# A list scheduler that hands out the lock between VectorE and GpSimd by turns

## The chip, the core and the metric

The kernel runs on one core of a Trainium2 chip. The core has five instruction queues: TensorE (PE), ScalarE (ACT), VectorE (DVE), GpSimd (POOL) and SyncE (SP); SP issues all DMA transfers here. Each queue is executed in the order in which it was written; between queues there are only semaphores. The time is the device time of one launch in microseconds. Each engine operates on tiles of 128 partitions; "128x512" is a tile of 512 float32 numbers in each partition.

## The reference

One encoder layer on a sequence of 2048 tokens with 1024 features, in float32. `mod` is six vectors from a conditioning vector c.

```python
mod = (silu(c) @ ada_w + ada_b)
sh1, sc1, g1, sh2, sc2, g2 = jnp.split(mod, 6, axis=-1)
h = rmsnorm(x, mix_norm_pre) * (1.0 + sc1) + sh1
y = windowed_gqa_sink(h, w_qkv, w_o, sink, rel_bias)     # 16 query heads, 4 key heads of 64
x = x + g1 * rmsnorm(y, mix_norm_post)
h = rmsnorm(x, ffn_norm_pre) * (1.0 + sc2) + sh2
a, b = jnp.split(h @ w_in, 2, axis=-1)                   # 2 x 2816
y = (silu(a) * b) @ w_out
x = x + g2 * rmsnorm(y, ffn_norm_post)
```

Attention works in blocks of 128 queries; each sees 384 keys (its own block and both neighbours), with a bias by relative position, and a learned extra logit in the softmax (the sink).

## The kernel before

**The work.** The sequence is cut into four chunks of 512 tokens (`NCH`), for the feed-forward part into two halves of 1024. Activations lie with features on partitions. A float32 matmul is made of three matmuls of the fp32r type: each operand is split into a high part (a cast by ACT, `hi`, or a cast of a weight, `w`) and a low part (the difference, mostly by DVE, `lo`), and high x high, high x low and low x high are added in one PSUM bank (`three`, `split`). So behind nearly each matmul of the kernel there are an ACT cast and a DVE subtraction of two inputs in SBUF.

The stages, in the order of time:

1. From 0 to about 170 us: the vectors of `mod` (40 loads `ada`, each reduced on DVE with `cb`, the broadcast conditioning vector), the norm of chunk 0, and the q, k, v projections of chunks 0 and 1. The normed input `x` becomes `hi` and `lo`; the weights are `wqkv` (raw) and `w`, or `wsr` and `ws` for the second part of the tiles.
2. To about 705 us: 64 attention units (score matmuls `bank<-k,q`, softmax on `pr` with running maximum `nm` and `rs`, value matmuls). Between them the scheduler places "fillers": the projections of chunks 2 and 3 (`fillers_qkv`), then the output projection (`fillers_o`, weights `wo`, activations `ol`) with residual and norm (`y`, `yacc`, `xacc`).
3. To about 800 us: the rest of the output projection. Results go to DRAM as `h2`; sums and differences of them (`hf`, written as `hd_d`) are operands of the next stage.
4. To about 1610 us: the hidden layer of the feed-forward part. Two by two blocks are multiplied in the manner of Strassen with seven products (`Block`, `Hidden`; `OPERANDS` names the blocks b11 to b22 and the sums t1 to t4 of the activations). Weights `wiri` are added up to `s_i` and split into `wa_i` and `ws_i`; results `p_i` and `u_i` are combined, partly on POOL.
5. To about 2050 us: the second matmul of the feed-forward part, again with seven products, in parts of 2 or 3 pairs of tiles (`PARTS`). Names end in `_o` here (`wiro`, `s_o`, `ws_o`, `wa_o`; `o1_0` is part 0 of half 1). The partial results are added up in the tiles `z`, partly by POOL. When the first half is complete, ACT squares its `z` (`zsq`), DVE adds the squares up (`zacc0` and `zacc1`, a chunk each), PE sums them over the partitions by a matmul with `ones` (`rstd_of`, named `nst`), and `zx` is written out.
6. The last chunks are normed and written (`finish`).

**The order.** The functions above don't issue instructions. Each call goes to a `Proxy`, and the `Recorder` (line 130) makes an `Op` of it, with its engine, the regions that it reads and writes, and its predecessors `pred`. `cost` (line 219) gives each `Op` a duration `occ` for its queue, a latency `lat` until its result may be used, and `port`, which says that it needs the lock which DVE and POOL share. `place` gives the tiles their addresses. `schedule` (line 537) then runs `ROUNDS` rounds. In each, `forward` (line 311) simulates the five queues with these durations: in a loop it takes the engine that can begin earliest, there the ready operation of the smallest `prio`, and adds it to the order; buffers of a tile go to the next that is to use them. An operation that needs the lock begins when the other engine's last locked operation has ended. From the second round on, an operation may be put back (up to four times, `o.put`) when a more urgent one, on its own engine or on the other side of the lock, will be ready before it would end. `backward` (line 477) takes the order of a round and works out the latest start of every operation, counted from the end; that is the `prio` of the next round. The round with the smallest simulated total is kept. `emit` (line 558) issues its order, inside `tc.manual_schedule()`, and the semaphores follow from the data alone. All instructions therefore have the line of `emit` in the profile, L594, and tiles tell them apart.

What `port` plans isn't enforced before: an order is fixed on each queue, but nothing says whether a DVE or a POOL operation goes first.

Of the kernel before, what the change touches and what calls it, by code (L numbers as in the profile page):

```python
# [19 lines left out]
P = 128  # L20
# [42 lines left out]

ROUNDS = 12

# [5 lines left out]

ENGINES = ("pe", "act", "dve", "pool", "sp")

class Op:
    __slots__ = ("i", "eng", "fn", "args", "kw", "reads", "writes", "occ", "lat", "port", "table", "tiles", "pred", "succ",
                 "start", "end", "put", "prio", "npred", "ready", "ins", "bytes")

# [52 lines left out]
class Recorder:  # L130
# [82 lines left out]
    def gap(self, q, op):  # L213

        if q.eng == op.eng == "pe":
            return 0
        return q.lat + (60 if q.eng != op.eng else 0)

    def cost(self, op, outs, ins):
# [6 lines left out]
        if eng == "sp":  # L226
            op.bytes = int(np.prod(outs[0].shape)) * 4
            op.occ, op.lat = 430, 0
        elif eng == "pe":
            if fn == "transpose":  # L230
                op.occ, op.lat = 108, 330
            elif outs[0].dtype == F32 and ins[0].dtype == F32:
                op.occ, op.lat = 860 * n // CH, 1060 * n // CH
            else:
                op.occ = n * 0.4167 + 13.5
                op.lat = op.occ + 200
        elif eng == "act":
            op.occ = n / 1.2 + (51 if psum else 93)
            op.lat = op.occ + 105
            if fn == "activation":  # L240
                if "accum_out" in op.kw:
                    op.occ, op.lat = op.occ + 93, op.lat + 93
                if isinstance(op.kw.get("scale"), bass.AP):
                    op.occ, op.lat = op.occ + 95, op.lat + 95
                f_ = op.args[2]
                op.table = {AF.Silu: "silu", AF.Ln: "log", AF.Exp: "log"}.get(f_)
        elif eng == "dve":
# [8 lines left out]
            if fn == "tensor_tensor_reduce":  # L256
                op.lat += 84
            op.port = n > P and (fast or len(sbuf) > 1)
        else:
            op.port = fn != "custom"  # L260
            if fn == "tensor_tensor":
                op.occ = n * 2.21 + 95
                op.lat = op.occ + 45
            elif fn == "custom":
                op.occ, op.lat = 1000, 1050
            else:
                op.occ = n * 1.05 + 153
                op.lat = op.occ + 35
# [42 lines left out]
    def forward(self, ahead):  # L311
# [8 lines left out]
        for o in ops:  # L320
            o.npred, o.ready, o.put = len(o.pred), 0.0, 0
# [3 lines left out]
        port = {"dve": 0.0, "pool": 0.0}  # L325
        lanes, dma, table = [0.0] * 8, 0.0, None
# [20 lines left out]
        def offer(o):  # L347
            ready = o.ready
            for b in o.tiles:
                if b.slot is None:  # L350
                    got = slot_of(b)
                    if got is None:
                        b.tag.parked.append(o)
                        return
                    ready = max(ready, got[1] + 60)
            heapq.heappush(soon[o.eng], (ready, o.prio, o.i, o))
# [18 lines left out]
        while n < len(ops):  # L375
            best = None
            for e in ENGINES:
# [18 lines left out]
            begin, e, o, src, item = best  # L396
            if e == "dve" and o.port and src is now[e] and begin > clock[e] + 150:
                other = [x for x in now[e] if not x[2].port]
                if other:
                    item = min(other)  # L400
                    o, begin = item[2], clock[e]
            if ahead and e in ("act", "dve", "pool") and o.put < 4:
                wait = 0.0
# [22 lines left out]
            for b in o.tiles:  # L426
                if b.slot is None:
                    got = slot_of(b)
                    if got is None:
                        again = True  # L430
                    elif got[1] + 60 > begin + 1e-6:
                        begin = got[1] + 60
# [18 lines left out]
            clock[e] = begin + o.occ  # L451
            o.start, o.end = begin, end
# [17 lines left out]
            for q in o.succ:  # L470
                q.npred -= 1
                q.ready = max(q.ready, begin if o.eng == q.eng == "pe" else end + (60 if o.eng != q.eng else 0))
                if not q.npred:
                    offer(q)
        return order, max(o.end for o in ops)

    def backward(self, order, total):


        after = {o: list(o.succ) for o in order}  # L480
        first = {}
        for o in order:
# [16 lines left out]
        late = {}  # L499
        lat = {o: o.lat if o.eng != "sp" else 2100 + o.bytes / 345.0 for o in order}  # L500
        for o in order:
# [3 lines left out]
        while left:  # L505
# [23 lines left out]
            for q in before[o]:  # L529
                g = 0 if q.eng == o.eng == "pe" else lat[q] + (60 if q.eng != o.eng else 0)  # L530
                limit[q] = min(limit[q], t - g + lat[q])
# [5 lines left out]
    def schedule(self, rounds):  # L537
# [6 lines left out]
        for i in range(rounds):  # L544
            order, total = self.forward(i > 0)
            if best is None or total < best[1]:
                best = order, total, {b: b.slot for b in self.bufs.values()}
# [5 lines left out]
        self.slots = best[2]  # L553
        return best[0]
# [3 lines left out]
    def emit(self, nc, tc, order, outside):  # L558
# [24 lines left out]
        banks = [nc.alloc_psum_tensor(f"bank{i}", [P, CH], F32).ap().tensor for i in range(BANKS)]  # L583
        table = None
        with tc.manual_schedule():
            for o in order:
# [6 lines left out]
                else:  # L593
                    getattr(engs[o.eng], o.fn)(*args, **kw)  # L594

# [1066 lines left out]
```

## Time and profile before

| | |
|---|---|
| median of three runs | 2072.3 us (2069.28 to 2074.15) |
| profiled execution | 2073.64 us, span 2071.9 us |
| mean granted clock of PE | 0.993 |
| busy PE, DVE, ACT, POOL | 2003.2, 1654.7, 1083.0, 744.2 us |
| instructions of PE, DVE, ACT, POOL in the profile | 9366, 2933, 2122, 687 |
| DMA | 396.35 MB, mean 191 GB/s |

An engine's busy time is the time in which it executes something. A row of a timeline gives the start, the length of a run of equal operations, what was done, and, in brackets, the idle time before it with the operation that ended the wait ("<-DVE ol" is the DVE operation that wrote `ol`). A DVE or POOL operation that waits for the lock appears in the trace as a longer operation and not as idle time. Tile names have their numbers left out.

### The profile page before, as it was taken

The page shows a single profiled execution, that of the slowest core. Times are in us where ns is not written, and L with a number is a line of the kernel's source. Part 1 is how long each engine was busy: PE and PEld are TensorE (multiplying, and loading weights), DVE is VectorE, ACT ScalarE, POOL GpSimd, SP SyncE. Part 2 cuts the span into 40 slices and gives each one's busy share as a digit, 9 for nine tenths or more (in the row PEclk, how much of TensorE's full clock was granted, in tenths as well). Part 3 has the DMA queues.
Part 4 walks back from the last instruction along what each step waited for, and adds up shares of the span by engine and source line. Part 5 has one row for each costly group of instructions (what it writes and reads, how often), then busy time and mean ns, then how long its engine had stood idle before and what let it go on. Part 6 is the DMA issues. An engine that isn't in the chain of part 4 may idle for free.

```text
span 2071.9 us, 29065 instructions
## 1 busy us (share of the span) xinstructions
PE 2003.2 (97%) x9366; PEld 1661.6 (80%) x9366; DVE 1654.7 (80%) x2933; ACT 1083.0 (52%) x2122; POOL 744.2 (36%) x687
## 2 busy tenths in 40 slices
PE   6999999999999999999999999999999999999997
PEld 4787888888778778788888888888888788877786
DVE  6666877765668889897988999776666789999998
ACT  5546776677778864343443533333334744465432
POOL 2403544466989723433445322222221000240031
PEclk9999999999999999999999999999999999999999
DMA  8896865676777794444456744423323544437443
GB/s 279 277 319 205 253 215 179 196 250 240 241 264 240 238 363 166 164 154 160 163 172 223 275 143 164 142 95 107 112 99 120 173 162 144 138 112 276 171 153 107
DMA packets 200516, 396.35 MB, mean 191 GB/s; under 512 B 20091, under 2 KB 62124, under 8 KB 195244
## 3 DMA queue, kind: packets, MB, share of 16 engines
q1 hardware_dynamic: 199788, 393.97, 56.6%
q8 instruction: 74, 1.21, 0.2%
q14 instruction: 78, 0.64, 0.1%
q10 hardware_dynamic: 576, 0.52, 0.1%
HBM read 270.65 MB, written 123.76 MB: 190 GB/s over the span
## 4 chain that ended last, share of the span: by engine, by line
PE 74%; DVE 12%; DMA 5%; ACT 3%; POOL 3%; issue 2%; SPq 1%; DVEq 0%; ACTq 0%; POOLq 0%
PE bank L594 74%; DVE z L594 3%; DMA ada<-ada_w 1%; SPq L594 1%; DVE ws_o L594 1%; POOL pr L594 1%; POOL y L594 1%; POOL z L594 1%; DMA zx<-x_d 1%; DVE ada L594 1%; DMA k_d<-e 1%; DVE wa_o L594 1%; DMA ol<-o_d 1%; DVE s_o L594 1%; DVE zacc L594 1%
## 5 line engine op out<-in xcount | busy, mean ns | idle before, releaser
L594 PE MATMUL bank<-ht,ws_i 128*128 128x512 f32 x1584 | 373.8, 389 | 0.0
L594 PEld LDWEIGHTS bank<-ht,ws_i 128*128 128x128 f32 x1584 | 297.3, 188 | 61.7
L594 PE MATMUL bank<-hb,wa_i 128*128 128x512 f32 x1056 | 254.2, 389 | 0.0
L594 PEld LDWEIGHTS bank<-hb,wa_i 128*128 128x128 f32 x1056 | 198.2, 188 | 41.4 <-ACT hb L594 0.2
L594 PE MATMUL bank<-ol,wo 128*128 128x512 f32 x768 | 206.6, 398 | 3.3 <-DVE ol L594 2.2
L594 POOL TENSOR_SCALAR pr<-pr,rs 128x384 f32<-128x384 f32 (+1 forms) x256 | 150.8, 607 | 126.2 <-DVE rs L594 122.2
L594 ACT ACTIVATE pr<-pr,nm 128x385 f32<-128x385 f32 (+1 forms) x256 | 155.0, 606 | 71.5 <-DVE nm L594 66.5
L594 ACT CAST ws_i<-s_i 128x512 fp32r<-128x512 f32 x132 | 82.0, 621 | 206.8 <-PE bank L594 129.7
L594 POOL TENSOR_TENSOR z<-z,z 128x512 f32<-128x512 f32 x32 | 63.3, 1999 | 349.6 <-issue 159.0
L594 DVE CUSTOM_DVE_ANT_0 pr<-bank,bias,nsink 128x384 f32<-128x384 f32 (+1 forms) x256 | 148.6, 596 | 44.4 <-PE bank L594 41.2
L594 POOL TENSOR_TENSOR p_i<-p_i,u_i 128x512 f32<-128x512 f32 x44 | 71.8, 1634 | 290.2 <-ACT wa_i L594 132.6
L594 DVE TENSOR_TENSOR u_i<-bank,u_i 128x512 f32<-128x512 f32 x176 | 120.6, 686 | 66.5 <-PE bank L594 65.9
L594 PEld LDWEIGHTS bank<-ol,wo 128*128 128x128 f32 x768 | 143.2, 189 | 30.7 <-DVE ol L594 2.6
L594 DVE TENSOR_TENSOR plo<-bank,phi 128x512 fp32r<-128x512 f32 x184 | 120.0, 685 | 37.4 <-ACT phi L594 35.3
L594 PE MATMUL bank<-k,q 128*128 128x384 f32 (+1 forms) x512 | 132.1, 345 | 5.3 <-DVE nm L594 5.2
L594 PE MATMUL bank<-hi,ws 128*128 128x512 f32 x384 | 137.1, 404 | 0.0
L594 ACT CAST wa_i<-wiri 128x512 fp32r<-128x512 f32 x132 | 81.4, 620 | 102.5 <-PE bank L594 102.2
L594 PE MATMUL bank<-hb,ws_i 128*128 128x512 f32 x528 | 128.7, 393 | 3.2 <-ACT p_i L594 3.2
L594 DVE TENSOR_TENSOR wa_i<-wiri,wa_i 128x512 fp32r<-128x512 f32 x132 | 113.8, 862 | 21.6 <-ACT wa_i L594 21.6
L594 PE MATMUL bank<-ht,wa_i 128*128 128x512 f32 x528 | 126.8, 389 | 0.0
L594 PEld LDWEIGHTS bank<-hb,ws_i 128*128 128x128 f32 x528 | 100.1, 190 | 25.0 <-ACT p_i L594 4.0
L594 PEld LDWEIGHTS bank<-ht,wa_i 128*128 128x128 f32 x528 | 99.1, 188 | 20.6
(245 smaller groups left out, 4511.8 us busy)
## 6 DMA issues: line engine op xcount, KB each, us to landing
wiri<-w_in SPq DMA_DIRECT2D x88, 512.0 KB, 4.7
ada<-ada_w SPq DMA_DIRECT2D x40, 512.0 KB, 5.5
wiro<-w_out SPq DMA_DIRECT2D x48, 384.0 KB, 3.7
q_d<-e SPq DMA_DIRECT2D x64, 256.0 KB, 3.8
q<-q_d SPq DMA_DIRECT2D x16, 1024.0 KB, 5.6
wo<-wo_d SPq DMA_DIRECT2D x16, 1024.0 KB, 6.2
g_d_b<-p_i SPq DMA_DIRECT2D x44, 256.0 KB, 4.7
g_d_t<-p_i SPq DMA_DIRECT2D x40, 256.0 KB, 2.0
```

The lines of the kernel that those rows point to most:

```text
L594: getattr(engs[o.eng], o.fn)(*args, **kw)
```

## The change

1. The lock in `forward`. Before, the engine that can begin first takes it. Now `ask` holds the time at which an operation would begin without the lock; among operations with the same `begin` the one that asked first is taken, so the two engines alternate when both wait. An operation may begin 60 ns ahead of the end of the other's.
2. Real dependences. An operation that is put back because of one on the other side of the lock remembers it (`o.wait = y`). If `y` has by then been scheduled and the operation would otherwise start no later than 20 ns after it, `o.extra = [y]`: its simulated start is after the end of `y`, and `emit` adds a dependence with `tc.add_manual_dep`, so that it waits for `y` by a semaphore. `backward` counts these edges too. In the built kernel there are 43 of them: in 31 a POOL operation waits for a DVE one, in 12 a DVE operation for a POOL one.
3. Durations and delays of the model. In place of 60 ns from one engine to another stand 55, 50, 35, 105 and 30 (`HOP`, by the waiting engine), and 30 within an engine. The latency of a matmul falls by 38; activations with a bias per partition get 95 more, POOL's additions 30 more, DVE's additions on 64 partitions 97 more. DMAs get a time on the wire by their bytes at 408 or 330 instead of 345 bytes per ns, issue times of 385 to 650 instead of 430, and a completion of 450 or 750 instead of 900; all clocks start at 700.
4. 18 rounds in place of 12. A method `replay` is added, which nothing calls.

The recorded operations and their counts on each engine are the same before and after (9352 on PE, 2935 on DVE, 1872 on ACT, 692 on POOL, 1228 on SP), and so is the arithmetic of each. The order differs: on DVE 1910 operations stand at another place in the queue (by 3.3 places in the mean, 65 at most), on PE 2064 (1.4, 156 at most), on ACT 942, on POOL 226 (11 at most) and on SP 660 (2.2, 32 at most).

```diff
-ROUNDS = 12
+ROUNDS = 18
+HOP = {"pe": 55, "act": 50, "dve": 35, "pool": 105, "sp": 30}
@@ gap
-        return q.lat + (60 if q.eng != op.eng else 0)
+        return q.lat + HOP[op.eng] if q.eng != op.eng else q.lat + 30
@@ cost
-            op.occ, op.lat = 430, 0
+            parts, run = outs[0].ap[0][1], min(self.run(x) for x in outs + ins)
+            op.wire = op.bytes / (0.408 if run >= 2048 and parts == P else 0.33) / 1e3
+            op.occ, op.lat = 650 if parts == DH or run * 2 * P == op.bytes else 385 if run >= 2048 else 450, 0
-                op.lat = op.occ + 200
+                op.lat = op.occ + 162
...
+            if outs[0].ap[0][1] == DH and fn == "tensor_tensor":
+                op.occ, op.lat = op.occ + 97, op.lat + 10
...
-                op.occ = n * 2.21 + 95
+                op.occ = n * 2.21 + 125
@@ forward
-        clock = dict.fromkeys(ENGINES, 0.0)
+        clock = dict.fromkeys(ENGINES, 700.0)
...
+                ask = begin
                 if o.port:
-                    begin = max(begin, port["pool" if e == "dve" else "dve"])
-                if best is None or begin < best[0]:
-                    best = begin, e, o, src, item
+                    begin = max(begin, port["pool" if e == "dve" else "dve"] - 60)
+                if best is None or (begin, ask) < best[:2]:
+                    best = begin, ask, e, o, src, item
...
-                            wait = max(wait, r + (y.occ if g != e else 1.0))
+                            w = r + (y.lat + HOP[e] if g != e else 1.0)
+                            if w > wait:
+                                wait, by = w, y if g != e else None
                 if wait:
                     drop(src, o)
                     o.put += 1
+                    if by is not None:
+                        o.wait = by
...
+            y = o.wait
+            if y is not None and y.npred < 0 and max(clock[e], o.ready) <= y.start + 20:
+                o.extra = [y]
+                begin = max(begin, y.end + HOP[e])
...
             if e == "sp":
                 lanes.sort()
                 begin = max(begin, lanes[0])
+                late = 150 * (lanes[3] > begin)
                 first = max(begin + 1200, dma)
-                dma = first + max(o.bytes / 345.0, 100.0)
-                end = dma + 900
+                dma = first + max(o.wire, 80.0) + {2: 500, 3: 1600}.get(moved, 0)
+                moved += 1
+                end = dma + (450 if o.out else 750)
...
@@ backward
+        for o in order:
+            for q in o.extra:
+                after[q].append(o)
@@ emit
+        sync = mybir.DependencyInfo(mybir.DependencyClass.Sync, mybir.DependencyReason.DATA)
...
+                for q in self.extra.get(o, ()):
+                    tc.add_manual_dep(o.ins.ins, q.ins.ins.name, sync, reason="turn")
```

More of the change, by code (lines that the diff above doesn't have):

```diff
@@ L450, in forward @@
                     port[e] = begin + o.occ
-            clock[e] = begin + o.occ
+            o.npred = -1
+            clock[e] = begin + o.occ + (late if e == "sp" else 0)
             o.start, o.end = begin, end
@@ L475, in forward, with replay @@
         return order, max(o.end for o in ops)
+    def replay(self, order):
+        queues = {e: [o for o in order if o.eng == e] for e in ENGINES}
+        at = dict.fromkeys(ENGINES, 0)
+        clock = dict.fromkeys(ENGINES, 700.0)
+        port, moved = {"dve": 0.0, "pool": 0.0}, 0
+        lanes, dma, table = [0.0] * 8, 0.0, None
+        after, seen = {}, set()
+        need = {}
+        for o in order:
+            o.npred, o.ready = len(o.pred), 0.0
+            edges = list(o.extra)
+            for b in o.tiles:
+                if b not in seen:
+                    seen.add(b)
+                    edges += [q for x in b.before for q in x.ops if q is not o]
+            o.npred += len(edges)
+            for q in edges:
+                after.setdefault(q, []).append(o)
+        n = 0
+        while n < len(order):
+            best = None
+            for e in ENGINES:
+                if at[e] == len(queues[e]):
+                    continue
+                o = queues[e][at[e]]
+                if o.npred:
+                    continue
+                begin = max(clock[e], o.ready, lanes[0] if e == "sp" else 0.0)
+                ask = begin
+                if o.port:
+                    begin = max(begin, port["pool" if e == "dve" else "dve"] - 60)
+                if best is None or (begin, ask) < best[:2]:
+                    best = begin, ask, e, o
+            begin, ask, e, o = best
+            at[e] += 1
+            if e == "act" and o.table and o.table != table:
+                table = o.table
+                begin += 1283
+            if e == "sp":
+                late = 150 * (lanes[3] > begin)
+                first = max(begin + 1200, dma)
+                dma = first + max(o.wire, 80.0) + {2: 500, 3: 1600}.get(moved, 0)
+                moved += 1
+                end = dma + (450 if o.out else 750)
+                lanes[0] = end
+                lanes.sort()
+            else:
+                end = begin + o.lat
+                if o.port:
+                    port[e] = begin + o.occ
+            clock[e] = begin + o.occ + (late if e == "sp" else 0)
+            o.start, o.end = begin, end
+            n += 1
+            for q in o.succ + after.get(o, []):
+                q.npred -= 1
+                q.ready = max(q.ready, begin if q.eng == e == "pe" else end + (HOP[q.eng] if q.eng != e else 30))
+        return max(o.end for o in order)
@@ L499, in backward @@
         late = {}
-        lat = {o: o.lat if o.eng != "sp" else 2100 + o.bytes / 345.0 for o in order}
+        lat = {o: o.lat if o.eng != "sp" else 1950 + o.wire for o in order}
         for o in order:
```

46 lines of the change are left out of this document (29 added, 17 removed).

## The prediction, made before the changed kernel was run

> **What bounds the kernel now.** I read the page's head first, then the chain that ended last, then the windows by stage, and last the timeline of TensorE (PE), because PE decides nearly everything here.
>
> ```profile
> span 2071.9 us, 29065 instructions
> PE 2003.2 (97%) x9366; PEld 1661.6 (80%) x9366; DVE 1654.7 (80%) x2933; ACT 1083.0 (52%) x2122; POOL 744.2 (36%) x687
> PE 74%; DVE 12%; DMA 5%; ACT 3%; POOL 3%; issue 2%; SPq 1%; DVEq 0%; ACTq 0%; POOLq 0%
> ```
>
> PE is busy 2003.2 of 2071.9 us, so all its idle time is 68.7 us. The change keeps every matmul; it can only shrink or enlarge that idle time and the stretches of lower clock that follow it. The windows show where it lies (columns: window, length, busy us and count of PE, PE weight loads, VectorE (DVE), ScalarE (ACT), GpSimd (POOL); granted clock; DMA share; GB/s):
>
> ```profile
> 0.00:50.00 50.00, 29.33 (x97) 19.77 (x98) 35.34 (x54) 25.52 (x34) 12.48 (x11) 1.00 0.80 278
> 150.00:200.00 50.00, 47.06 (x212) 38.84 (x211) 33.36 (x69) 34.09 (x69) 14.65 (x18) 0.93 0.70 223
> 550.00:600.00 50.00, 44.72 (x218) 35.83 (x218) 31.31 (x76) 37.54 (x82) 46.87 (x51) 0.97 0.71 236
> 700.00:750.00 50.00, 46.71 (x207) 37.53 (x206) 39.81 (x42) 31.74 (x48) 23.53 (x15) 1.00 0.97 347
> 800.00:850.00 50.00, 47.84 (x204) 39.09 (x203) 44.78 (x54) 18.17 (x32) 24.71 (x16) 0.97 0.46 163
> 1800.00:1850.00 50.00, 49.85 (x220) 40.97 (x219) 47.73 (x87) 30.20 (x61) 19.66 (x5) 1.00 0.48 159
> 1850.00:1900.00 50.00, 41.88 (x168) 31.75 (x168) 45.99 (x74) 34.04 (x64) 4.80 (x4) 0.97 0.74 256
> 1900.00:1950.00 50.00, 47.62 (x210) 39.11 (x210) 47.96 (x89) 22.92 (x46) 0.00 (x0) 1.00 0.55 191
> ```
>
> The startup loses 20.67 us of PE time. After it, five stages lose something: 150 to 200 (2.94), 550 to 600 (5.28), 700 to 750 (3.29), 800 to 850 (2.16) and 1850 to 1950 (8.12 + 2.38). From 1800 on DVE is busy 46 to 48 of 50 us, so there it stands next to PE as a bound. The waits themselves, in the timeline of PE (start, us, work; in brackets the idle time before it and who ended it):
>
> ```profile
> 24.28 2.08 PE L594 MATMUL bank<-hi,w 128*128 128x512 f32 x4 [9.26 <-ACT hi L594]
> 175.86 0.80 PE L594 MATMUL bank<-k,q 128*128 128x256 f32 x2 [2.70 <-DVE nm L594]
> 573.32 0.62 PE L594 MATMUL bank<-k,q 128*128 128x384 f32 x2 [2.27 <-DVE nm L594]
> 728.94 1.40 PE L594 MATMUL bank<-ol,wo 128*128 128x512 f32 x5 [2.25 <-DVE ol L594]
> 840.18 4.61 PE L594 MATMUL bank<-hb,ws_i 128*128 128x512 f32 x12 [2.15 <-ACT p_i L594]
> 862.15 3.04 PE L594 MATMUL bank<-hb,ws_i 128*128 128x512 f32 x12 [1.00 <-ACT p_i L594]
> 1858.01 2.07 PE L594 MATMUL bank<-zacc,ones 128*128 128x512 f32 x2 [3.27 <-DVE zacc L594]
> 1893.06 2.11 PE L594 MATMUL bank<-ht2o,ws_o 128*128 128x512 f32 x8 [1.82 <-ACT z L594]
> 1924.35 0.73 PE L594 MATMUL bank<-hb11o,wa_o 128*128 128x512 f32 x2 [2.38 <-ACT wa_o L594]
> ```
>
> The same twelve matmuls take 4.61 us after the wait at 840 and 3.04 us after the one at 862: some waits are followed by a slow stretch, worth 1.6 us there. The windows' clock agrees: (1 - 0.97) x 50 = 1.5 us in three of them, (1 - 0.93) x 50 = 3.5 us in 150 to 200.
>
> **The change, part by part.** It removes and adds no instruction. Every engine issues the same operations in another order, and 43 dependences are new: 31 times a POOL operation waits for a DVE one, 12 times the reverse. The order of the built kernels gives the moves used below. The other edits (18 rounds, new delays and durations in the planner's model, the unused `replay`) have no cost on the chip beyond the order that they lead to. So I go stage by stage, with each price bounded by idle plus slow clock from the rows above.
>
> *Startup.* These rows are of ACT and PE:
>
> ```profile
> 22.76 0.81 ACT L594 ACTIVATE x<-x,mod,coef 128x512 f32<-128x512 f32 x1 [4.87 <-DVE coef L594]
> 23.61 0.62 ACT L594 CAST hi<-x 128x512 fp32r<-128x512 f32 x1
> 27.42 0.94 ACT L594 CAST w<-wqkv 128x896 fp32r<-128x896 f32 x1 [0.37 <-DMA wqkv<-w_qkv]
> 34.28 1.89 PE L594 MATMUL bank<-lo,w 128*128 128x512 f32 x7 [1.42 <-DVE lo L594]
> 49.42 1.20 PE L594 MATMUL bank<-lo,w 128*128 128x512 f32 x4 [1.17 <-DVE lo L594]
> 55.96 1.20 PE L594 MATMUL bank<-lo,w 128*128 128x512 f32 x4 [1.49 <-DVE lo L594]
> 61.58 1.20 PE L594 MATMUL bank<-lo,w 128*128 128x512 f32 x4 [0.54 <-DVE lo L594]
> ```
>
> The new ACT order has the casts of weights w0_1 and w0_2 ahead of the first scaled activation x0_0 and its cast to `hi`. The cast at 27.42 is w0_2; it waited for its DMA. If that weight lands when it does now, `hi` ends at 27.42 + 0.94 + 0.81 + 0.62 = 29.8 instead of 23.61 + 0.62 = 24.2: PE starts 5.6 later. The head of the queue thus blocks x0_0, hi0_0 and the first matmul behind it. But four later waits, 1.42 + 1.17 + 1.49 + 0.54 = 4.6 us, are for data that arrive at their own pace, and they shrink by as much: net +1.0. On DVE three operations of the modulation (`ada`) move ahead of the norm, which frees their buffers and lets SP issue the next loads earlier. If the weights then land before ACT wants them, PE starts as now and the four waits go: -4.6. If nothing is absorbed, it is +5.6. I take +1.0, since weight and waits are both measured.
>
> *173 us.* ACT stands on one cast:
>
> ```profile
> 172.65 1.05 ACT L594 CAST ws<-wsr 128x1024 fp32r<-128x1024 f32 x1 [5.00 <-DMA wsr<-w_qkv]
> 175.06 0.50 ACT L594 ACTIVATE pr<-pr,nm 128x257 f32<-128x257 f32 x1
> ```
>
> For 5.00 us this cast of ws8 waited for its DMA, with two softmax activations queued behind it, and PE's scores behind these. The new order puts both activations and one `e` ahead of it. The wait of 2.70 should go but for one softmax activation of 0.50: -2.2. I keep the slow clock, as nothing shows it gone. Ends: 0 (the DMA is as late and something else stands behind it) and -(2.70 + 3.5) = -6.2.
>
> *566 to 616 us.* One row of DVE, for the price of an operation without contention:
>
> ```profile
> 832.55 0.68 DVE L594 TENSOR_TENSOR s_i<-wiri 128x512 f32<-128x512 f32 x1
> ```
>
> POOL is busy 46.87 of 50 us, with the same operations afterwards. A better order cannot lift that; four of the new edges (y, yacc) make POOL wait for a DVE operation here. Four times 0.68 would be +2.7; the other end is all idle and slow clock, -(5.28 + 1.5) = -6.8. I take -1.0, near zero, because the bound stays.
>
> *711 to 732 us.* PE waits for `ol`, whose load was issued late:
>
> ```profile
> 719.42 0.89 SPq L594 DMA_DIRECT2D ol<-o_d  x1
> 717.25 1.78 DVE L594 TENSOR_TENSOR hf<-y,hf 128x512 f32<-128x512 f32 x1
> 724.57 1.05 ACT L594 CAST ol<-ol 128x1024 fp32r<-128x1024 f32 x1 [1.63 <-DMA ol<-o_d]
> ```
>
> SP issues in order, and the load of ol3_3 stood behind writes of `h2` and `hd_d_t`, whose sources come from DVE operations stretched to 1.78 us. In the new SP order it stands seven places earlier, ahead of these writes; DVE's own part stands eight places earlier. Eight operations of 0.68 are 5.4 us, more than the 2.25 that PE waits, so the wait goes; the writes are then late, and no one on PE reads them soon. -2.3; ends 0 and -3.3 (all idle of the window).
>
> *825 to 862 us.* Here DVE and POOL take turns already:
>
> ```profile
> 829.14 1.78 DVE L594 TENSOR_TENSOR wiri<-wiri 128x512 f32<-128x512 f32 x1
> 830.33 1.75 POOL L594 TENSOR_TENSOR ly<-ly,lr 128x512 f32<-128x512 f32 x1
> ```
>
> This row of DVE is the last of three alike from 825.75 on: 1.78 instead of 0.68 made DVE 3.3 late, and through weights and casts `p_i` was late at 840 and 862. The planner now foresees this and two of the new edges (ly2_2, wa12_i0_5 after POOL operations) lie here. Ends: -(2.15 + 1.00 + 1.5) = -4.7, and two more such turns, 2 x 1.1 = +2.2. I take -2.0, a little nearer to the gain, the weight splits having been moved for it.
>
> *1835 to 1925 us.* This is the largest pool after the startup:
>
> ```profile
> 1835.42 14.71 POOL L594 TENSOR_TENSOR z<-z,z 128x512 f32<-128x512 f32 x2 [10.47 <-DVE z L594]
> 1847.18 0.55 DVE L594 TENSOR_TENSOR wiro<-wiro 128x384 f32<-128x384 f32 x1
> 1848.91 1.15 ACT L594 ACTIVATE zsq<-z 128x512 f32<-128x512 f32 x2 [2.63 <-POOL z L594]
> 1924.92 1.09 PE L594 MATMUL bank<-ht2o,ws_o 128*128 128x512 f32 x4
> 1925.85 0.39 PE L594 MATMUL bank<-hb11o,wa_o 128*128 128x512 f32 x1
> ```
>
> POOL's first `z` was ready at 1835.42, and the two took 14.71 us where one takes 1.75 above: DVE ran weight splits without a pause until 1847.7 and only then did POOL end. From there the way is POOL z, ACT zsq, DVE zacc, then PE's norm matmul with 3.27 idle. In the new order the two sums zacc end 25 and 31 places earlier on DVE, with the splits of o1_0_2 and o1_0_3 behind them, and the norm matmul stands 64 matmuls earlier on PE (the last two rows put four matmuls at 0.93 us, 0.23 each, and 64 at 14.7). Ends: -(8.12 + 2.38 + 1.5) = -12.0 when the chain flows, and 14.7 less the 1.82 at 1893 that it would absorb = +12.9 when `z` comes as late as now and PE stands at the earlier place. I take -3.0: the wait of 3.27 goes, and those up to 1925 stay, since DVE is as full as before.
>
> The sum is 1.0 - 2.2 - 1.0 - 2.3 - 2.0 - 3.0 = -9.5. The profiled execution took 2073.64 us, 1.3 above the median of the three runs (2072.3); 2073.64 - 9.5 = 2064.1, and against the median 2062.8.
>
> [...]
>
> **The rivals.**
>
> *First, slower: the norm chain is starved at its new place.* POOL's `z` must win the lock between DVE operations that stand back to back; at 1835 it lost for over 12 us. DVE now has zacc between splits and, standing in order, would itself stop until `z` is through, at 47.73 of 50 us busy. PE's norm matmul is fixed 14.7 us earlier. It decides when `z` is over 5 us late there. Price +12.9 in place of -3.0: 2062.8 + 15.9 = 2078.7. For it speaks the row at 1835; against it that the new edges give POOL's z0_1_5 and z0_3_4 a fixed place behind a DVE operation, and that DVE leaves the lock free while it waits for zsq.
>
> *Second: the startup's delay isn't absorbed.* Then +5.6 in place of +1.0: 2067.4. For it speaks that the ACT queue is in order; against it the four waits of 4.6.
>
> *Third: the new waits take back what the moves give.* 43 edges at 0.68 are 29 us, at 1.78 they are 77. DVE and POOL carry 12 + 3 = 15% of the chain that ended last, so some 4.4 to 11.5 us lie on the path: 2067.2 to 2074.3, in the middle 2071, no change that can be measured. For it speaks that a wait between full engines is seldom free; against it that POOL is 36% busy overall and most of its edges are in the hidden stage, where PE loses little.
>
> **How the numbers follow.** A measurement of this kernel tells about 0.2% (4.1 us) from no change, so "same" is 2068.2 to 2076.4. Forecast (2056 to 2068): 0.38. First rival (2076 to 2084): 0.22. Second (2065 to 2071): 0.12, of which 0.05 faster and 0.07 same. Third (2067 to 2079): 0.28, of which 0.03 faster, 0.12 same and 0.13 slower. Faster 0.46, same 0.19, slower 0.35. The range 2053 to 2082 leaves some 0.08 at each side; the forecast's own is 2056 to 2068.
>
> **What would show it.** Right: the first matmul near 29 us and shorter waits for `lo` until 62; no 5 us wait of ACT for wsr near 173; no `ol` wait at 729; POOL's `z` of 1.3 to 1.8 us each near 1835 and the norm matmul without idle time. Wrong: PE's idle time above 68.7 us, a `z` of POOL over 5 us with PE waiting behind zacc, or POOL waits in 550 to 620 longer than now.

## The result, and the profile after

The changed kernel takes 2088.3 us (median; 2085.7 to 2089.1), the kernel before 2073.2 us (2069.3 to 2075.7): a ratio of 1.0071, with a 95% interval of 1.0058 to 1.0084. It is slower by 15 us (0.7%), where 10 us faster had been forecast. The profiled execution took 2085.66 us, 12.0 more than the one of before (2073.64); its span is 11.6 longer.

The head of the page after, and the shares of its chain:

```profile
span 2083.5 us, 29084 instructions
PE 2003.7 (96%) x9366; PEld 1664.8 (80%) x9366; DVE 1639.4 (79%) x2933; ACT 1082.6 (52%) x2122; POOL 726.0 (35%) x687
PE 71%; DVE 10%; DMA 10%; issue 3%; ACT 2%; POOL 2%; SPq 1%; DVEq 0%; ACTq 0%; POOLq 0%
```

PE does the same work, so its idle time grew from 68.7 to 79.8 us. DVE and POOL are busy for 15.3 and 18.2 us less, 33.5 us together, with the same operations. A wait for the lock counts as busy time: before, 128x512 operations of DVE from 825.75 to 829.14 us, beside POOL's, took 1.76 to 1.78 us, and 0.68 at 832.55, with POOL idle; the ends of the two engines' operations alternate there (DVE 827.51, POOL 828.67, DVE 829.21, POOL 830.37). By these sums the engines wait less for each other: the change does on them what it says. But the share of DMA in the chain that ended last has doubled, from 5% to 10%. The windows of after (columns as in the prediction):

```profile
150.00:200.00 50.00, 41.99 (x183) 34.34 (x182) 32.94 (x64) 32.83 (x63) 13.81 (x15) 0.93 0.81 255
550.00:600.00 50.00, 44.80 (x212) 35.66 (x211) 29.47 (x73) 34.71 (x75) 45.84 (x50) 0.90 0.65 225
700.00:750.00 50.00, 46.59 (x215) 37.68 (x214) 38.62 (x51) 37.57 (x65) 25.72 (x22) 0.97 0.81 287
850.00:900.00 50.00, 47.04 (x200) 38.00 (x199) 39.16 (x54) 17.94 (x30) 22.52 (x16) 0.97 0.44 149
1850.00:1900.00 50.00, 39.92 (x161) 31.22 (x161) 43.40 (x76) 29.70 (x57) 3.33 (x2) 0.93 0.66 219
1900.00:1950.00 50.00, 50.00 (x223) 41.39 (x222) 49.80 (x92) 25.64 (x54) 0.00 (x0) 1.00 0.56 202
```

The window from 150 to 200 lost 5 us more of PE time than before (41.99 busy against 47.06). The one from 550 to 600 is as idle as before, but at a clock of 0.90 instead of 0.97. From 1850 to 1900 more is lost and from 1900 to 1950 all is regained. The timeline of PE, with the waits that matter:

```profile
28.14 0.79 PE L688 MATMUL bank<-hi,w 128*128 128x512 f32 x1 [14.06 <-ACT hi L688]
88.60 0.47 PE L688 MATMUL bank<-nhia,ones 128*128 128x512 f32 x1 [2.75 <-DVE nhia L688]
169.39 0.39 PE L688 MATMUL bank<-k,q 128*128 128x256 f32 x1 [2.43 <-DVE e L688]
176.63 0.58 PE L688 MATMUL bank<-k,q 128*128 128x256 f32 x1 [5.58 <-DVE nm L688]
583.28 1.01 PE L688 MATMUL bank<-k,q 128*128 128x384 f32 x2 [2.27 <-DVE nm L688]
723.63 1.64 PE L688 MATMUL bank<-ol,wo 128*128 128x512 f32 x6 [3.26 <-DMA wo<-wo_d]
798.53 0.50 PE L688 MATMUL bank<-nhilo,ones 128*128 128x512 f32 x1 [1.73 <-DVE nhilo L688]
895.37 0.49 PE L688 MATMUL bank<-nhil,ones 128*128 128x512 f32 x1 [2.10 <-DVE nhil L688]
1856.09 0.70 PE L688 MATMUL bank<-zacc,ones 128*128 128x512 f32 x1 [2.25 <-DVE zacc L688]
1878.02 1.22 PE L688 MATMUL bank<-hb11o,wa_o 128*128 128x512 f32 x2 [7.41 <-ACT wa_o L688]
```

Both kernels issue the same number of matmuls, so the start of the n-th one can be compared in the two traces (the first has number 0). That places the loss without asking which wait is whose:

| n-th matmul | before, us | after, us | later by |
|---|---|---|---|
| 300 | 94.19 | 95.51 | 1.3 |
| 600 | 152.66 | 154.11 | 1.4 |
| 900 | 219.94 | 226.58 | 6.6 |
| 2550 | 530.31 | 538.35 | 8.0 |
| 3000 | 625.93 | 636.59 | 10.7 |
| 3600 | 748.11 | 759.15 | 11.0 |
| 4200 | 889.50 | 902.90 | 13.4 |
| 7500 | 1639.70 | 1651.66 | 12.0 |
| 8700 | 1926.98 | 1939.75 | 12.8 |
| 9364 (last but one) | 2058.80 | 2070.35 | 11.6 |

The largest step, 5.2 us, is the start of the attention between 150 and 220 us, where a wait was expected to vanish. These rows of ACT, POOL and DVE of after lead to PE's wait of 5.58:

```profile
156.35 0.58 ACT L688 CAST e<-bank 128x512 fp32r<-128x512 f32 x1 [3.65 <-DMA q_d<-e]
172.27 1.33 ACT L688 ACTIVATE nsq<-x 128x512 f32<-128x512 f32 x2 [1.37 <-DMA x<-xT]
172.97 1.26 POOL L688 TENSOR_TENSOR nacc<-nacc,nsq 128x512 f32<-128x512 f32 x1 [3.11 <-ACT nsq L688]
174.27 0.69 DVE L688 TENSOR_TENSOR nacc<-nacc,nsq 128x512 f32<-128x512 f32 x1 [2.56 <-POOL nacc L688]
176.09 0.48 DVE L688 CUSTOM_DVE_ANT_0 pr<-bank,bias,nsink 128x256 f32<-128x256 f32 x1
```

At 156 ACT stands for 3.65 us, because the buffer `e` (there are two) is still being written out to `q_d`. The operations on the second half of chunk 2 stand behind it and release the buffers for the loads of chunk 3 later. At 172 ACT waits for the last of these loads; its square goes to POOL's sum and then to DVE's, and only behind that sum in DVE's queue stands `pr`, the softmax step which also gives the maximum `nm` that PE's next score matmul waits for. The cast of `ws8` that held ACT before isn't in this chain any more.

The same chain stood in the kernel before, 5 to 6.5 us earlier; ACT waited there for `q_d` too, for longer, but at 140 us:

```profile
140.33 0.60 ACT L594 ACTIVATE e<-bank 128x512 fp32r<-128x512 f32 x1 [4.47 <-DMA q_d<-e]
167.03 0.63 ACT L594 ACTIVATE nsq<-x 128x512 f32<-128x512 f32 x1 [0.93 <-DMA x<-xT]
167.76 0.69 DVE L594 TENSOR_TENSOR nacc<-nacc,nsq 128x512 f32<-128x512 f32 x1 [1.67 <-ACT nsq L594]
```

So what changed first is when the transfers come, and not how long they take in a crowd. The view of DMA (issues, KB each, median us from issue to landing) shows it: its stretch from 144 to 157 us of after, from 134 to 146 us of before, and from 130 to 145 us of e10, the fastest kernel of those below.

```profile
DMA packets 3248, 4.92 MB, mean 378 GB/s; under 512 B 181, under 2 KB 2460, under 8 KB 3247
bias<-tab_d SPq DMA_DIRECT2D x3, 768.0 KB, 9.0
k_d<-e SPq DMA_DIRECT2D x4, 256.0 KB, 7.7
q_d<-e SPq DMA_DIRECT2D x2, 256.0 KB, 8.9
```

```profile
bias<-tab_d SPq DMA_DIRECT2D x4, 768.0 KB, 8.1
q_d<-e SPq DMA_DIRECT2D x5, 256.0 KB, 7.6
```

```profile
bias<-tab_d SPq DMA_DIRECT2D x4, 768.0 KB, 7.5
q_d<-e SPq DMA_DIRECT2D x2, 256.0 KB, 10.0
```

The bias loads, 768 KB each, were issued from 134.6 us on before, from 142.7 us on after, and from 129.7 us on in e10. The writes around and behind them are slow in all three (`q_d` 7.6, 8.9 and 10.0 us, against 3.7 in the median of the whole kernel of after). Before, this crowd was ending when the loads of chunk 3 and the writes of k came, from 148.5 us on; these then took 4.1 and 4.4 us:

```profile
k_d<-e SPq DMA_DIRECT2D x7, 256.0 KB, 4.4
x<-xT SPq DMA_DIRECT2D x6, 256.0 KB, 4.1
```

After, the writes of k fall into it, and the last load of chunk 3 is issued at 168.76 us instead of 163.24.

Over the whole kernel, by the last part of the page of after, the medians are

```profile
wiri<-w_in SPq DMA_DIRECT2D x88, 512.0 KB, 4.7
q_d<-e SPq DMA_DIRECT2D x64, 256.0 KB, 3.7
wo<-wo_d SPq DMA_DIRECT2D x16, 1024.0 KB, 5.9
g_d_t<-p_i SPq DMA_DIRECT2D x40, 256.0 KB, 2.0
```

Worked out from the code for a transfer with nothing ahead of it, the figures that the planner holds against the first three are:

| | 256 KB write | 512 KB load | 1024 KB load |
|---|---|---|---|
| before (345 bytes per ns, 900 ns) | 2.9 | 3.6 | 5.1 |
| changed (408 or 330, 450 or 750 ns) | 2.4 | 3.2 | 4.5 |
| median in the trace of after | 3.7 | 4.7 | 5.9 |
| tried below (300, 1500 ns) | 3.6 | 4.4 | 6.2 |

Against these three medians both models are too short, and the change makes the DMA part worse. But what a transfer takes depends on its place here (writes of 256 KB landed in 8.9 us in the stretch of `q_d` above, in 3.7 in the median of all `q_d`, and those of `g_d_t` in 2.0, in both kernels), and the planner also puts one transfer behind another (`first = max(begin + 1200, dma)`), so this is no direct comparison. The fairer test is the whole plan. Its own total, which the planner's code gives when it is run, is 2033.1 us for the changed kernel and 2025.4 for the one before: the traces' spans are 50 and 46 us longer. In e10 (300 bytes per ns and 1500 ns) it is 2053.9, and the span 7 us longer. The changed kernel's plan has the four bias loads land 6.4 to 9.8 us after their issue, as in the trace (6.5 to 9.8). What it has wrong there is the time: the first is issued at 126.1 us in the plan and at 142.7 in the trace (before 124.0 and 134.6, in e10 130.8 and 129.7).

### The profile page after: what moved, and what is told of

Its sections match the earlier page's. It is cut to its first block, busy times and chain, and to the rows that moved or that the text cites. A ratio compares the mean times of both kernels' runs of the same rounds, so it can differ in the third digit from the quotient of the medians.

```text
span 2083.5 us, 29084 instructions
## 1 busy us (share of the span) xinstructions
PE 2003.7 (96%) x9366; PEld 1664.8 (80%) x9366; DVE 1639.4 (79%) x2933; ACT 1082.6 (52%) x2122; POOL 726.0 (35%) x687
## 4 chain that ended last, share of the span: by engine, by line
PE 71%; DVE 10%; DMA 10%; issue 3%; ACT 2%; POOL 2%; SPq 1%; DVEq 0%; ACTq 0%; POOLq 0%
PE bank L688 71%; DVE z L688 2%; DMA q_d<-e 2%; DMA ada<-ada_w 1%; SPq L688 1%; DMA o_d<-of 1%; DMA wqkv<-w_qkv 1%; DVE zx L688 1%; DMA hd_d_t<-hf 1%; DVE u_i L688 1%; DVE ada L688 1%; DVE ws_o L688 1%; POOL w L688 0%; DMA x<-xT 0%; DVE wa_o L688 0%
## 5 line engine op out<-in xcount | busy, mean ns | idle before, releaser
L688 POOL TENSOR_TENSOR z<-z,z 128x512 f32<-128x512 f32 x32 | 47.4, 1500 | 361.7 <-ACT wa_o L688 154.6
L688 PE MATMUL bank<-hi,w 128*128 128x512 f32 x320 | 105.6, 407 | 17.1 <-ACT hi L688 17.1
```

The source lines that it names most:

```text
L688: o.ins = getattr(engs[o.eng], o.fn)(*args, **kw)
```

## The experiments

Three theories stood against each other. A: the planner's new DMA times are too short, so its orders lean on transfers that come later, and the engines stand still at them, as ACT did for 3.65 us at 156. B: the turns, that is, the waits between VectorE and GpSimd, cost the time. C: any edit deals another order, and no part is to blame. The timings (the median of before lies between 2072.4 and 2075.5 us in them, so the ratio compares better than the time):

| run | DMA figures | turns | us | ratio to before, 95% |
|---|---|---|---|---|
| changed kernel | new | yes | 2088.3 | 1.0058 to 1.0084 |
| e1, without the 43 dependences | new | order only | 2089.5 | 1.0047 to 1.0077 |
| e8, 106 ns | new | yes | 2084.6 | 1.0035 to 1.0073 |
| e4, old lock | new | no | 2101.2 | 1.0102 to 1.0136 |
| e5, DMA figures alone | new | no | 2099.6 | 1.0108 to 1.0147 |
| e11, old completion | new rate, 900 ns | yes | 2076.6 | 1.0002 to 1.0026 |
| e2, old DMA figures | old | yes | 2078.1 | 0.9999 to 1.0018 |
| e3, lock alone | old | yes | 2074.6 | 0.9981 to 0.9999 |
| e12, lock alone, 61 ns | old | yes | 2071.3 | 0.9982 to 1.0002 |
| e6, delays and durations alone | old | no | 2081.6 | 1.0027 to 1.0057 |
| e7, 61 ns | old | no | 2081.1 | 1.0031 to 1.0058 |
| e9, lock alone, slow DMA | slow | yes | 2066.8 | 0.9956 to 0.9980 |
| e10, changed, slow DMA | slow | yes | 2063.4 | 0.9939 to 0.9972 |
| e13, as e10, 106 ns | slow | yes | 2072.0 | 0.9973 to 0.9994 |
| e14, before, slow DMA | slow | no | 2069.3 | 0.9960 to 0.9985 |

**e1: the same order without the added waits.**

```diff
-                for q in self.extra.get(o, ()):
+                for q in ():
                     tc.add_manual_dep(o.ins.ins, q.ins.ins.name, sync, reason="turn")
```

> The changed kernel with the same order on every queue, but without the 43 added dependences. Theory A (the planner's new DMA times are too short, so orders lean on loads and writes that come later, and the in-order queues stand still): the order is what costs, so 2086 to 2090 us, PE still idle near 88, 169 and 176 us. Theory B (the turns: waits between VectorE and GpSimd cost the time): 2073 to 2080 us. Theory C (any edit of the planner's figures deals another order, and its time spreads by some 10 us either way, with no single part to blame): 2086 to 2090 us as for A, since the order is the same.

2089.5 us, as slow as the changed kernel (2088.3). The 43 waits cost nothing that can be measured; the order does. B falls in its direct form. The waits aren't without effect either: without them DVE and POOL are busy for longer (1639.4 and 726.0 us with them):

```profile
PE 2006.7 (96%) x9366; PEld 1665.0 (80%) x9366; DVE 1646.1 (79%) x2933; ACT 1082.8 (52%) x2122; POOL 730.4 (35%) x687
```

**e2 and e4: one part of the change undone.** e2 puts the DMA model of before back:

```diff
-            op.wire = op.bytes / (0.408 if run >= 2048 and parts == P else 0.33) / 1e3
-            op.occ, op.lat = 650 if parts == DH or run * 2 * P == op.bytes else 385 if run >= 2048 else 450, 0
+            op.wire = op.bytes / 345.0
+            op.occ, op.lat = 430, 0
...
-                dma = first + max(o.wire, 80.0) + {2: 500, 3: 1600}.get(moved, 0)
-                end = dma + (450 if o.out else 750)
+                dma = first + max(o.wire, 100.0)
+                end = dma + 900
```

> The changed kernel with the DMA model of the kernel before (345 bytes per ns, 430 ns per issue, 900 ns to completion), all else new: lock by turns, dependences, delays, durations, 18 rounds. Theory A: the losses up to 200 us go, 2073 to 2080 us. Theory B: 2085 to 2091 us. Theory C: any time from 2065 to 2095 us, and the losses up to 200 us need not go.

2078.1 us, a ratio of 1.0008 (0.9999 to 1.0018): most of the loss is gone by this part alone. A's time came, but not where it said: the 900th matmul starts at 225.68 us, nearly as late as in the changed kernel (226.58). In their traces, what e2 gains lies between the 2550th matmul (537.67 against 538.35) and the 4200th (894.40 against 902.90).

e4 puts the lock of before back:

```diff
-                    begin = max(begin, port["pool" if e == "dve" else "dve"] - 60)
-                if best is None or (begin, ask) < best[:2]:
+                    begin = max(begin, port["pool" if e == "dve" else "dve"])
+                if best is None or begin < best[0]:
...
-            if y is not None and y.npred < 0 and max(clock[e], o.ready) <= y.start + 20:
+            if False and y is not None and y.npred < 0 and max(clock[e], o.ready) <= y.start + 20:
```

(and `y.occ` without the delay in `w`).

> The changed kernel with the lock as before (no turns, no added dependences), all other edits kept. Theory A: 2083 to 2091 us, with losses of some 6 us against the kernel before by 200 us. Theory B: 2070 to 2078 us. Theory C: 2065 to 2095 us.

2101.2 us, even slower than the changed kernel. In this pair of orders the turns gain 13 us; how much of that an order gives by chance is asked below. The groups of instructions of e4 show POOL's `z` as slow as before, and slower (1999 ns in the mean before; 1500 after; 2116 here):

```profile
L688 POOL TENSOR_TENSOR z<-z,z 128x512 f32<-128x512 f32 x32 | 67.0, 2116 | 358.6 <-DVE z L688 190.2
```

This holds for all runs: the mean of these `z` is 1916 to 2120 ns in the six kernels planned without turns and 1467 to 1563 in the ten with them.

**e3, e5 and e6: one part alone on the kernel before.** e3 has the turns and the dependences and no other edit; e5 the DMA figures (and the start at 700); e6 `HOP` and the durations of the engines.

> The kernel before with the lock by turns and the added dependences alone (44 of them here); DMA model, delays, durations, start and 12 rounds are those of before. Theory A: 2070 to 2078 us. Theory B: 2083 to 2090 us, with longer waits of POOL and VectorE for each other. Theory C: 2065 to 2095 us.

> The kernel before with the new DMA model alone (and all clocks starting at 700): lock, delays, durations and 12 rounds of before, no added dependences. Theory A (the new DMA times are too short): 2083 to 2092 us, with waits for loads and writes. Theory C (any edit deals another order, spread of some 10 us, no part to blame): 2065 to 2095 us.

> The kernel before with the new delays between engines and the new durations of PE, ACT, VectorE and POOL, without the new DMA model and without turns or dependences. Theory A: 2070 to 2078 us, nothing in it is about DMA. Theory C: 2065 to 2095 us. If it is slow without turns and e2, which has the turns as well, is not, the turns give back what the new durations cost.

Against before, measured along with them, e3 is all but unchanged (2074.6 us), e5 27 us slower (2099.6) and e6 9 slower (2081.6). Only e5 goes far beyond the others, so the harm is in the DMA figures, as A says. In e5 the score matmul waits longer still:

```profile
182.26 0.80 PE L687 MATMUL bank<-k,q 128*128 128x256 f32 x2 [6.42 <-DVE nm L687]
```

**e7, e8 and e12: what an edit without a meaning does.** 61 for 60 ns on the kernel before (e7), 106 for 105 ns of `HOP` towards POOL on the changed one (e8), 61 for 60 in e3 (e12).

```diff
-        return q.lat + (60 if q.eng != op.eng else 0)
+        return q.lat + (61 if q.eng != op.eng else 0)
```

> A control for theory C: the kernel before with 61 in place of 60 ns from one engine to another, nothing else. The edit means nothing, but it deals another order. Theory A: 2069 to 2078 us. Theory C: off by 5 us or more from 2073 in either direction; if it is, single differences of that size between the variants prove nothing.

> The same control on the changed kernel: 106 in place of 105 ns of delay towards POOL, nothing else. Theory A: 2084 to 2092 us, as the DMA model stays. Theory C: off by 5 us or more from 2088 in either direction.

> The lock by turns and the dependences alone (as e3), with 61 in place of 60 ns: the partner of e7, which has 61 ns and no turns and took 2081 us. If the turns help by themselves: 2066 to 2077 us. If they do nothing: 2076 to 2086 us. If e3 was a lucky deal: above 2080 us.

One ns costs the kernel before 8.7 us (2081.1), and moves the changed one to 2084.6 and e3 to 2071.3, some 3 to 4 us each. So C is right in part: the order of before is rather a lucky one, and differences under some 10 us between two planners prove nothing. In e7 the attention starts as badly as in the changed kernel:

```profile
180.42 0.79 PE L594 MATMUL bank<-k,q 128*128 128x256 f32 x2 [7.11 <-DVE nm L594]
```

e6's 9 us can be no more than such a deal. Nor does that wait alone set the time: e12 has one of 7.01 us at 173.66 and takes 2071.3 us.

**e9, e10, e11, e13 and e14: DMA figures the other way.** e10 changes only this in the changed kernel (the planner's backward pass gets the same), e13 is e10 with 106 for 105 ns, e9 is e3 with it, e14 the kernel before with it; e11 takes only the old completion.

```diff
-            op.wire = op.bytes / (0.408 if run >= 2048 and parts == P else 0.33) / 1e3
+            op.wire = op.bytes / 300.0
...
-                end = dma + (450 if o.out else 750)
+                end = dma + 1500
```

> The planner of before with turns and dependences, and a DMA model moved the other way: 300 bytes per ns and 1500 ns to completion (345 and 900 before), which puts a load of 512 KB at 4.4 us and one of 1024 KB at 6.2 us, near the medians of the profile (4.7 and 5.6 to 6.2). Theory A (short DMA times cost the time): 2060 to 2073 us, faster than before. Theory C (each edit deals another order, no part to blame): 2065 to 2095 us.

> The changed kernel with the same two figures only (300 bytes per ns, 1500 ns to completion in place of 408 or 330 and 450 or 750); new issue times, delays, durations, turns, dependences and 18 rounds stay. Theory A: 2066 to 2079 us, at least 9 us below the changed kernel. Theory C: 2075 to 2100 us, no order among e2, e10 and the changed kernel.

> The changed kernel with the completion of before alone (900 ns in place of 450 for writes to DRAM and 750 for loads); bytes per ns and issue times stay new. Theory A, if the completion is what is too short: 2074 to 2082 us as in e2; if it is the rate of 408 bytes per ns: 2084 to 2092 us. Theory C: 2075 to 2100 us.

> e10 with 106 in place of 105 ns of delay towards POOL, nothing else: another order from the same DMA figures (300 bytes per ns, 1500 ns). If the DMA figures are the cause: 2060 to 2072 us, and again no loss between 150 and 200 us. If e10 was a lucky deal: 2075 us or more.

> The kernel before (no turns, no dependences, old delays and durations, 12 rounds) with 300 bytes per ns and 1500 ns to completion alone. If short DMA times are what costs, with or without turns: 2062 to 2073 us, below e7's 2081. If the turns are needed for it: 2075 to 2085 us.

All four kernels with slow DMA figures are faster than before: 2063.4, 2066.8, 2069.3 and 2072.0 us (e13 barely, its interval ends at 0.9994). The five with the whole new DMA model (the changed one, e1 in the same order, e4, e5 and e8) take 2084.6 to 2101.2, those with the old one 2071.3 to 2081.6 (before itself 2072 to 2075). By their ratios the three groups don't overlap, although each holds kernels with and without turns, and with old and new durations: this shows that the DMA figures decide. The edges are close: e8 and e7 have 1.0054 and 1.0044, e3 and e13 0.9990 and 0.9984. With 900 ns for the completion alone (e11) most of the loss is gone, though the rate of 408 stays; that is one deal, and the rate alone wasn't tried. e13 shows the luck in e10, 8.6 us; it is still 16 us below the changed kernel. The turns aren't needed for it (e14). In each of the five pairs that differ by the turns (before and e3, e7 and e12, e14 and e9, e4 and the changed kernel, and, with six rounds more, e6 and e2) the kernel with turns has the lower ratio, by 0.0004 to 0.0052; e7's deal alone is worth 0.0044, so a small gain of the turns is likely but not shown.

Why the figures decide is in part argued. The plans with the new figures end 50 to 72 us before the traces' spans, those with the old ones 38 to 54 and those with the slow ones 7 to 24: group by group, the nearer the plan is to the chip, the faster its order, which is what A says. But the completion also sets how long one of the planner's eight places for transfers in flight is taken (`lanes`), so the slow figures let fewer be planned at a time; no run takes the two apart.

e10 is the fastest, at 0.9955 of the time of before (0.9939 to 0.9972). Its page, its chain and its first window of the attention:

```profile
PE 2001.5 (97%) x9366; PEld 1664.1 (81%) x9366; DVE 1636.5 (79%) x2933; ACT 1079.1 (52%) x2122; POOL 721.1 (35%) x687
PE 87%; DVE 6%; POOL 2%; ACT 2%; issue 2%; DMA 2%; SPq 0%; DVEq 0%; ACTq 0%; POOLq 0%
150.00:200.00 50.00, 48.97 (x239) 40.38 (x238) 37.66 (x82) 38.36 (x81) 17.10 (x23) 1.00 0.89 274
```

DMA has 2% of the chain instead of 10%, and PE is busy for 48.97 us of the window instead of 41.99, at full clock. The 900th matmul starts at 209.80 us, 16.8 earlier than in the changed kernel and 10.1 earlier than before; 6.0 and 4.7 of that were gained in the startup, by the 300th (89.48 us). No score matmul of e9, e10, e13 or e14 waits for over 1 us between 155 and 195 us. In each of the others one waits for 1.8 to 7.7 us there. This is the part of A that holds at its place. What limits e10 now stands at other places, and the wait for `wa_o` behind the norm is there as in the changed kernel (7.41 at 1878), so it doesn't come from the DMA figures alone:

```profile
831.59 0.73 PE L688 MATMUL bank<-hb,ws_i 128*128 128x512 f32 x2 [4.16 <-ACT p_i L688]
1855.18 1.22 PE L688 MATMUL bank<-hb11o,wa_o 128*128 128x512 f32 x2 [6.53 <-ACT wa_o L688]
```

Not tried: lower rates or longer completions than these, the issue times and the start at 700 apart from the rest of the DMA figures, and a second deal of most planners. The 18 rounds play no part in the changed kernel: the round that it keeps is the ninth.

## Why the prediction was wrong

By its own steps, with the delays of the table of matmuls (the change of "later by" between two rows):

| step | forecast | measured |
|---|---|---|
| startup (to the 300th matmul) | +1.0 | +1.3 |
| 173 us (600th to 900th) | -2.2 | +5.2 |
| between the stages looked at (900th to 2550th) | 0 | +1.4 |
| 566 to 616 us (2550th to 3000th) | -1.0 | +2.6 |
| 711 to 732 us (3000th to 3600th) | -2.3 | +0.4 |
| 825 to 862 us (3600th to 4200th) | -2.0 | +2.4 |
| 1616 us (4200th to 7500th) | 0 | -1.4 |
| 1835 to 1925 us (7500th to 8700th) | -3.0 | +0.8 |
| end | 0 | -1.2 |

- *Startup: the mechanism right, the size with luck.* The two casts do stand ahead, PE's first such matmul starts at 28.14 (29 to 30 forecast, 24.28 before), and the four waits for `lo` until 62 us are gone. That the sum fits is luck, as two terms of it were off: the start is 3.9 us late instead of 5.6, and waits for `hi` of 2.47 and 0.58, which weren't priced, stand where those for `lo` were.
- *173 us: wrong, and the largest miss.* It was right that the cast of ws8 no longer holds the softmax. The step that failed is "The wait of 2.70 should go but for one softmax activation": it asked only what stood ahead of the scores on ACT, and took the sum of chunk 3, behind which `nm` stands on DVE, to come when it did. That sum came at 174.27 instead of 167.76, and the step measured +5.2 instead of -2.2. The bias loads, now 8 us later, stand among the transfers that free `e` and load chunk 3; that they are what makes the sum late is argued from the times of these transfers. The prediction had the DMA's lateness as an end of its range at 0; a loss was not in it.
- *566 to 616 us.* POOL stayed the bound (45.84 of 50), as said. The loss is in the clock, 0.90 instead of 0.97: (0.97 - 0.90) x 50 = 3.5 us, over a stretch with no more idle time. A change of the clock had no term of its own.
- *711 us.* The wait for `ol` is gone, as forecast; the next operand, `wo`, is late by 3.26. "The writes are then late, and no one on PE reads them soon" asks for the writes behind the moved load, and not for the loads beside it; that the move made `wo` late isn't shown.
- *825 to 862 us.* The waits for `p_i` shrank as forecast, and the matmuls of norms (`nhilo`, `nhil`), which stand 3 and 13 places earlier on PE, now wait for 1.73 and 2.10 us.
- *1835 us.* The starvation of POOL, priced as the first rival, didn't come: the largest `z` of POOL there is one of 2.07 us, and the wait for zacc fell from 3.27 to 2.25.

```profile
1833.13 5.66 POOL L688 TENSOR_TENSOR z<-z,z 128x512 f32<-128x512 f32 x4 [8.12 <-DVE z L688]
1851.52 2.07 POOL L688 TENSOR_TENSOR z<-z,z 128x512 f32<-128x512 f32 x1 [12.74 <-DVE z L688]
```

  The weight splits that were put behind the norm, which the prediction names and doesn't price, became a wait for `wa_o` of 7.41 at 1878; it ate the gain and what the later waits gave back.

What failed in common is the sum itself: it took the known waits away one by one, and set every place without a wait at zero. Here an order in which thousands of operations moved made more waits than it removed. In kind that is nearest to the third rival, in which the change takes back what the moves give, but neither in size (it gave 2067 to 2079) nor in its mechanism, since e1 shows that the added waits cost nothing. And the part of the change that decided, the DMA figures, was set aside with "no cost on the chip beyond the order that they lead to", a term put at nothing, although the landing times of the page before, 3.8 and 4.7 us for 256 and 512 KB, stood against the planner's 2.4 and 3.2. From them the loss could at least have been made a rival. What they led to is the difference between 2088.3 us and e2's 2078.1 or e10's 2063.4.

The turns show on the chip, and mostly by the order: POOL's `z` fell from 1999 to 1500 ns in the mean with the turns, and to 1512 in e1, where only the order holds them.

## What to carry to other kernels

Where a planner orders the work, compare its plan with the trace, first of all the times of its transfers: here the shorter ones went with 2084.6 to 2101.2 us, and times longer than before cost nothing (e9, e10, e13 and e14). Judge a planner by several deals of it (a constant changed by 1 ns), since one order against one order differed by up to 9 us here for no reason. And when an order changes as a whole, don't add up the waits that go: look at which resource will be late next on each queue, DMA's included.

## What the runs showed of the hardware

- A DVE operation on one element per partition took 2.07 us beside one of POOL, no less than the 1.78 of 128x512 beside POOL at 829.14 of before. The rows of after, DVE's `coef` and POOL's `w`:

```profile
33.57 2.07 DVE L688 SCALAR_TENSOR_TENSOR coef<-mod,gains 128x1 f32<-128x1 f32 x1
33.23 2.40 POOL L688 TENSOR_TENSOR w<-wqkv,w 128x896 fp32r<-128x896 f32 x1 [4.35 <-ACT w L688]
```

  It ends within 0.01 us of POOL's (35.64 and 35.63); at 22.57 and 24.04 us of before, with POOL idle, `coef` took 0.15 and 0.16. The planner takes such operations (`n > P` in `cost`) for free of the lock.
- When 4.92 MB passed in 13 us at 378 GB/s (144 to 157 us of after), landings of 256 KB, of `k_d` and `q_d`, took 7.7 and 8.9 us in the median, against 3.7 for `q_d` over the whole kernel. Writes of 256 KB among loads of 768 KB were about as late as these (8.9 and 9.0 us).
- The same idle time in a stretch can go with different clocks: from 550 to 600 us PE was busy for 44.72 us before and 44.80 after, at a granted clock of 0.97 and 0.90. What decides between them isn't shown here.
